# Two-layer encoder trunk on one core: start of the first block, order of the weight casts, pace of the linear heads, last residual

## The chip, the core and the metric

The kernel runs on one core of a Trainium2 chip. A time is the device time of one execution in microseconds (us). The numbers shown for the kernel before are the median of three runs and one execution that was profiled. TensorE is called PE, VectorE DVE, ScalarE ACT, GpSimd POOL and SyncE SP, as the profile calls them. SP, POOL and ACT issue the DMA transfers.

## The reference

Two layers of the same form act on x (512 tokens by 2048, float32):

```python
def hybrid_layer(x, w_in, w_out, g_pre, g_post, w_alpha, b_alpha, g_gla, g_att, rel_bias):
    h = rmsnorm(x, g_pre)
    z = h @ w_in
    gq, gk, gv, gg, ga, aq, ak, av, ag = split_columns(z)
    log_a = log_sigmoid(ga @ w_alpha + b_alpha) / GLA_TAU
    o_gla = gla_chunk_causal(gq, gk, gv, log_a)       # 4 linear heads, state per chunk of 64 tokens
    o_gla = rmsnorm(o_gla, g_gla) * silu(gg)          # norm per head
    o_att = chunk_band_attention(aq, ak, av, rel_bias)
    o_att = rmsnorm(o_att, g_att) * silu(ag)
    y = concatenate([o_gla, o_att]) @ w_out
    return x + rmsnorm(y, g_post)
```

w_in is 2048 by 7184 and w_out 2048 by 2048 for each layer, all float32. The matmuls with w_in and w_out are nearly all of the work.

## The kernel before

**Tiles.** The weights are cut into blocks of 512 output columns, and a block into 8 chunks of 256 rows of the inner dimension, 512 KB each. A chunk lands in a tile `raw` or `H` (two halves of 128 rows side by side: 128 x 1024). Each operand is held as two rounded parts, a high and a low one. ACT makes the high part `wh` of a weight chunk (line 203, a cast), DVE the low part `wl = raw - wh` (line 207); for activations `split` does the same at lines 108 (ACT) and 109 (DVE). A product is then three matmuls: high by high, high by low, low by high. A group of matmuls adds up in a PSUM tile `mm` of 128 x 512.

**Blocks.** `std_gemm` (matmuls at line 323) multiplies a block plainly: gate columns of the attention heads (AG0, AG1) at the start of a layer, and three passes over output blocks at the end of it (NB_IN with four output tiles of 128 tokens; NB_IN+1 in two passes of two tiles). The other blocks go in pairs through `fast_gemm` (lines 399, 409): seven products P1 to P7 of sums of sub-blocks in place of eight. The sums of activations for these are made by `make_sums` (DVE, line 604), split (lines 108, 109), and go through memory. W23 is the pair of output blocks that stands between the two passes over NB_IN+1. It needs the sums of the heads' outputs.

**Weights ahead.** `stream` is the list of all chunks in the order of use. `ahead()` is called when a chunk's matmuls have been written down, and prepares chunks that come later: the load, the cast (`high`) and the subtraction (`low`) of the third chunk on, and the load and cast of the fourth. `wl` has three buffers, `wh` and `raw` four.

**Order.** Each engine runs its own list of instructions in order. The lists are made from the program as written, by a scheduler that moves instructions within their dependencies; `tc.issue_after(x)` adds that an instruction comes behind x. Side work (heads, sums, residuals) is written as generators in `tasks`; the matmul loops advance them by `pump`, `rate` steps for each chunk of matmuls.

**Start.** The transposed input (`in_xt`, tiles H and g, 256 KB each) and the first chunk of AG0 come by SP's queue, two small tables (`gcol`, `cst`) by ACT's. Ten matmuls on zeros (line 654) run on PE until the first operands are there.

**Gates.** When an AG block's sum is complete, ACT reads it from PSUM, scales it by the token's norm and applies SiLU (line 694). The next block's sums use the same PSUM tiles.

**Linear heads.** After the value pair (GV0, GV1) `gla_heads` runs, for four heads and two halves of the tokens: state updates (`outer`, PE, line 1060), reads of the state (`read`, PE, line 1094), sums of squares and norm (`norm`: ACT line 1104, then the power on POOL, line 447), scaling by norm and gate on DVE (line 1112, `gate`), transposition on PE (line 1122, `turn`), scaling by column on ACT (line 1133), and the split into the operand of the output block (tiles a12x, g16, g17, g4, g5). NB_IN takes these operands chunk by chunk; the last two chunks of it need the heads that come last.

**Ends of output blocks.** `project` reads a finished sum: squares on ACT (line 1239), product with the gain on DVE (line 1242). `finish_token` adds up the squares, takes the norm and adds the residual (lines 1255 to 1270). For the last 128 tokens the residual is cut into four pieces of 512: three on DVE (line 1268), one on ACT and POOL (lines 1264, 1265); their stores go out by the queues of SP and ACT in turn.

The functions that the change touches, with their line numbers before it:

## Time and profile before

| what | value |
| --- | --- |
| median of 3 runs | 1643.76 us (1642.11 to 1644.25) |
| profiled execution, its own time | 1642.16 us |
| its span | 1640.4 us |
| PE busy | 1623.6 us, 99% of the span |
| DVE busy | 1227.6 us, 75% |
| ACT busy | 905.5 us, 55% |
| POOL busy | 178.2 us, 11% |
| moved by DMA | 469.59 MB, 286 GB/s on average |

The span runs from the first to the last instruction of the profiled execution; 1.76 us of that execution's time lie outside it. Rows of the timeline give start, duration, engine, line, operation, output<-input, shapes, and in brackets how long the engine had been idle and what ended it. Matmuls overlap: one of 128 x 512 shows some 0.39 us in the trace, while the next one starts some 0.23 us after it.

### The profile page before, as it was taken

How to read it: one execution, taken by the hardware profiler on the slowest of the kernel's cores; microseconds unless marked ns; L12 is line 12 of the kernel's file. 1: busy time of each engine (PE TensorE's matmuls, PEld its weight loads, DVE VectorE, ACT ScalarE, POOL GpSimd, SP SyncE). 2: the span in 40 equal slices, each digit the busy share in tenths (PEclk: the TensorE clock that was granted, in tenths of full speed). 3: DMA queues.
4: the chain of work that ended last, by engine and by line, in shares of the span. 5: the costliest groups of instructions: out<-in, count | busy, mean ns of one | idle time of the engine just before them, and what ended most of it. 6: DMA issues, size and time to landing. Idle time of an engine off the chain costs nothing.

```text
span 1640.4 us, 24886 instructions
## 1 busy us (share of the span) xinstructions
PE 1623.6 (99%) x9030; PEld 1392.1 (85%) x9030; DVE 1227.6 (75%) x1579; ACT 905.5 (55%) x1515; POOL 178.2 (11%) x259
## 2 busy tenths in 40 slices
PE   9999999999999999999999999999999999999997
PEld 7888889999988877688888888899999888776886
DVE  7567776877877876678776676768778778857887
ACT  7444544556666644455784445445556765445553
POOL 1210000001101201310132000000001001013111
PEclk9999999999999999999999999999999999999999
DMA  9979796958858696899779797968588676967996
GB/s 380 350 273 320 281 313 228 309 173 309 293 179 297 206 383 211 283 370 357 285 257 383 267 338 258 322 220 302 192 310 271 207 271 232 357 230 287 394 327 226
DMA packets 150490, 469.59 MB, mean 286 GB/s; under 512 B 16396, under 2 KB 35604, under 8 KB 150368
## 3 DMA queue, kind: packets, MB, share of 16 engines
q1 hardware_dynamic: 127632, 389.36, 68.3%
q0 software_dynamic: 22016, 77.37, 12.1%
q8 instruction: 71, 1.16, 0.3%
q10 hardware_dynamic: 720, 1.28, 0.2%
q14 instruction: 51, 0.42, 0.1%
HBM read 395.83 MB, written 71.06 MB: 285 GB/s over the span
## 4 chain that ended last, share of the span: by engine, by line
PE 97%; DVE 1%; DMA 1%; ACT 1%; issue 0%; DVEq 0%; POOL 0%; SPq 0%; ACTq 0%; POOLq 0%
PE mm L409 45%; PE mm L323 21%; PE mm L399 20%; PE ax L890 2%; PE ax L409 1%; PE ax L873 1%; PE ax L1060 1%; PE ax L721 1%; PE ax L1094 1%; PE ax L853 1%; PE ax L852 1%; PE ax L851 1%; DMA t<-fg 0%; PE ax L921 0%; PE ax L551 0%
## 5 line engine op out<-in xcount | busy, mean ns | idle before, releaser
L409 PE MATMUL mm<-wh,sa 128*128 128x512 f32 x1536 | 484.6, 391 | 0.1
L203 ACT CAST wh<-raw 128x1024 fp32r<-128x1024 f32 x256 | 270.1, 1056 | 262.9 <-PE mm L409 113.3
L207 DVE TENSOR_TENSOR wl<-raw,wh 128x1024 fp32r<-128x1024 f32 x256 | 312.6, 1222 | 122.6 <-PE mm L323 39.0
L203 ACT CAST wh<-H 128x1024 fp32r<-128x1024 f32 x224 | 235.5, 1053 | 221.4 <-PE mm L409 115.1
L207 DVE TENSOR_TENSOR wl<-H,wh 128x1024 fp32r<-128x1024 f32 x224 | 273.8, 1223 | 109.0 <-PE mm L409 50.4
L409 PEld LDWEIGHTS mm<-wh,sa 128*128 128x128 f32 x1536 | 288.0, 188 | 62.3 <-issue 2.4
L409 PE MATMUL mm<-wl,sa 128*128 128x512 f32 x768 | 300.3, 391 | 0.1
L399 PE MATMUL mm<-sa,wh 128*128 128x256 f32 x1280 | 237.1, 285 | 0.0
L399 PEld LDWEIGHTS mm<-sa,wh 128*128 128x128 f32 x1280 | 199.9, 191 | 0.3
L409 PE MATMUL mm<-wh,a 128*128 128x512 f32 x576 | 186.3, 393 | 0.0
L399 PE MATMUL mm<-sa,wl 128*128 128x256 f32 x640 | 180.6, 283 | 0.0
L323 PE MATMUL mm<-wh,a 128*128 128x512 f32 x512 | 167.9, 394 | 4.0 <-ACT a L108 1.2
L409 PEld LDWEIGHTS mm<-wl,sa 128*128 128x128 f32 x768 | 144.2, 188 | 29.6 <-DVE wl L207 0.5
L447 POOL TENSOR_TENSOR sm<-sm,mhalf 128x4 f32<-128x4 f32 (+2 forms) x40 | 67.1, 1678 | 767.1 <-DVE sm L906 542.0
L197 DVE TENSOR_TENSOR H<-H,raw 128x1024 f32<-128x1024 f32 x120 | 146.5, 1221 | 1.7
L409 PEld LDWEIGHTS mm<-wh,a 128*128 128x128 f32 x576 | 108.0, 188 | 22.5
L399 PEld LDWEIGHTS mm<-sa,wl 128*128 128x128 f32 x640 | 122.3, 191 | 0.1
L323 PEld LDWEIGHTS mm<-wh,a 128*128 128x128 f32 x512 | 96.0, 188 | 27.5 <-DVE g L1242 2.0
L409 PE MATMUL mm<-wl,a 128*128 128x512 f32 x288 | 112.9, 392 | 0.0
L323 PE MATMUL mm<-wl,a 128*128 128x512 f32 x256 | 100.4, 392 | 0.5 <-DVE wl L207 0.5
L399 PE MATMUL mm<-a,wh 128*128 128x256 f32 x512 | 94.7, 285 | 0.0
L323 PE MATMUL mm<-wh,sa 128*128 128x512 f32 x256 | 87.0, 396 | 0.0
(203 smaller groups left out, 2324.8 us busy)
## 6 DMA issues: line engine op xcount, KB each, us to landing
raw<-in_w_dram SPq DMA_DIRECT2D x320, 512.0 KB, 5.6
sa<-S SPq DMA_DIRECT2D x192, 512.0 KB, 4.7
H<-in_w_dram SPq DMA_DIRECT2D x56, 512.0 KB, 4.7
sa<-A SPq DMA_DIRECT2D x48, 512.0 KB, 6.5
S<-g POOLq DMA_DIRECT2D x32, 512.0 KB, 7.7
oS<-g POOLq DMA_DIRECT2D x32, 512.0 KB, 6.3
sa<-oS SPq DMA_DIRECT2D x32, 512.0 KB, 5.5
sg<-t POOLq DMA_DIRECT2D x32, 256.0 KB, 5.7
```

Source lines behind the costliest of these rows:

```text
L197: nc.vector.tensor_tensor(out=h, in0=h, in1=r, op=ALU.add)
L203: last_cast[0] = nc.scalar.copy(self.wh, src).ins
L207: last_low[0] = nc.vector.tensor_tensor(out=self.wl, in0=self.src, in1=self.wh.bitcast(F32), op=ALU.subtract).ins
L323: mm = nc.tensor.matmul(pss[o], a[:, part, t], rhs[:, kk, :], start=(i == 0 and kk == 0 and m == 0), stop=(i == n - 1 and kk == 1 and m == 2),
L399: nc.tensor.matmul(dst, lhs[:, kk, f], a[:, part, tok], start=(fresh and kk == 0 and m == 0 and ft % 2 == 0), stop=(c == c_last and kk == ...
L409: nc.tensor.matmul(out_ps[t], a[:, part, tok], rhs[:, kk, :], start=(fresh and kk == 0 and m == 0), stop=(c == c_last and kk == 1 and m == ...
L447: return nc.gpsimd.tensor_tensor(out=out_r, in0=v, in1=mhalf[:, : v.shape[-1]], op=ALU.pow).ins
L721: nc.tensor.matmul(ps[0:96, half * 256 : (half + 1) * 256], wga[kt // 10][:, kt % 10, :], op[:, i, (kt % 2) * 256 : (kt % 2 + 1) * 256], s ...
L851: nc.tensor.matmul(ps[:, :n], self.qh[:, t], self.kh[:, :n], start=True, stop=False)
L852: nc.tensor.matmul(ps[:, :n], self.qh[:, t], self.kl[:, :n], start=False, stop=False)
L853: nc.tensor.matmul(ps[:, :n], self.ql[:, t], self.kh[:, :n], start=False, stop=True)
L890: nc.tensor.matmul(o, self.pt[i][:, j * P : (j + 1) * P], av[hd // 4, j // 2][:, j % 2, (hd % 4) * P : (hd % 4 + 1) * P], start=(j == 0), ...
```

## The change

The changed kernel differs in five places.

1. **First chunk.** The first weight chunk of AG0 is loaded as two halves of 128 x 512. DVE casts the first half, ACT the second, and the subtraction is in two halves too. The table `cst` is loaded by SP's queue behind the first chunk's loads, not by ACT's.
2. **Casts behind gates.** Gate functions return their last instruction, and `high` writes every later cast behind it (`issue_after(last_evac[0])`). Output blocks return nothing, so nothing is added there.
3. **Two chunks ahead.** In `ahead()` the cast and subtraction of plain blocks (`std`) are prepared one chunk later than before: two chunks ahead (casts three, in the second round).
4. **Linear heads.** The pair (GV0, GV1) advances the side work by 4 steps per chunk of matmuls, before 2.
5. **Last residual.** The last 128 tokens' residual is cut into pieces of 512, 512, 512, 256 and 256, all on DVE.

No arithmetic changes; PE has the same matmuls.

```diff
     LEFT = {"P5": "S1", "P6": "S2", "P3": "S4", "P7": "S3", "P4": "A22"}
+    last_evac = [None]
...
             if k == "std":
                 i = done["load"]
-                if i < NCH:
+                if i == 0:
+                    self.raw = rtile("raw")
+                    load_columns(i, 0)
+                    parts = w[self.l, b0, c].rearrange("p (k n) -> p k n", k=2)
+                    for kk in range(2):
+                        with tc.issue_after(last_load[0]):
+                            last_load[0] = nc.sync.dma_start(self.raw[:, kk, :], parts[:, kk, :]).ins
+                    load_columns(i, 1)
+                elif i < NCH:
...
             self.wh = rtile("wh", dtype=F32R)
-            last_cast[0] = nc.scalar.copy(self.wh, src).ins
+            if done["high"] == 0:
+                nc.vector.tensor_copy(self.wh[:, 0, :], src[:, 0, :])
+                last_cast[0] = nc.scalar.copy(self.wh[:, 1, :], src[:, 1, :]).ins
+                return
+            with tc.issue_after(last_evac[0]) if last_evac[0] else nullcontext():
+                last_cast[0] = nc.scalar.copy(self.wh, src).ins
 
         def low(self):
             self.wl = rtile("wl", dtype=F32R, bufs=3)
-            last_low[0] = nc.vector.tensor_tensor(
-                out=self.wl, in0=self.src, in1=self.wh.bitcast(F32), op=ALU.subtract
-            ).ins
+            for kk in range(2) if done["low"] == 0 else (slice(0, 2),):
+                last_low[0] = nc.vector.tensor_tensor(
+                    out=self.wl[:, kk, :], in0=self.src[:, kk, :], in1=self.wh[:, kk, :].bitcast(F32), op=ALU.subtract
+                ).ins
...
         for what, n in (("load", 3), ("high", 3), ("low", 3), ("load", 4), ("high", 4), ("load", 5)):
+            if what != "load" and all(z.kind == "std" for z in stream[i + n - 2 : i + n]):
+                n -= 1
             prepare(what, i + n)
...
             if i == n - 1:
                 last_mm = mm.ins
-                evac(o, pss[o])
+                last_evac[0] = evac(o, pss[o])
                 closing[0] = last_mm
...
     nc.scalar.dma_start(gcol, g_cols)
-    nc.scalar.dma_start(cst, consts)
+    prepare("load", 1)
+    with tc.issue_after(last_load[0]):
+        last_load[0] = nc.sync.dma_start(cst, consts).ins
     prepare("load", 4)
...
         def gate(half, q, t, src, scale=1.0):
             dst = t2()
-            nc.scalar.activation(dst, src, AF.Silu, scale=scale)
+            made_gate = nc.scalar.activation(dst, src, AF.Silu, scale=scale).ins
             nc.gpsimd.dma_start(sg_d[l][half][t * P : (t + 1) * P, q * W : (q + 1) * W], dst)
+            return made_gate
...
-                gate(half, q, o, ps, inv_rms(l, o))
+                return gate(half, q, o, ps, inv_rms(l, o))
...
-        fast_gemm(l, PAIRS[5], gv_consume, rate=2, after=fetch_operands)
+        fast_gemm(l, PAIRS[5], gv_consume, rate=4, after=fetch_operands)
...
-            step = 512 if end else xs[0].shape[-1]
-            for i in range(D // step):
-                h, o = i * step // 1024, i * step % 1024
-                xt, yt = piece(xs, i * step, step), ys[t, h][:, o : o + step]
-                if end and i == 3:
-                    nc.scalar.activation(yt, yt, AF.Copy, scale=r)
-                    nc.gpsimd.tensor_tensor(out=xt, in0=yt, in1=xt, op=ALU.add)
-                else:
-                    with tc.issue_after(last_low[0]):
-                        nc.vector.scalar_tensor_tensor(out=xt, in0=yt, scalar=r, in1=xt, op0=ALU.mult, op1=ALU.add)
+            o = 0
+            for i, n in enumerate((512, 512, 512, 256, 256) if end else (xs[0].shape[-1],) * (D // xs[0].shape[-1])):
+                xt, yt = piece(xs, o, n), ys[t, o // 1024][:, o % 1024 : o % 1024 + n]
+                with tc.issue_after(last_low[0]):
+                    nc.vector.scalar_tensor_tensor(out=xt, in0=yt, scalar=r, in1=xt, op0=ALU.mult, op1=ALU.add)
                 q = (nc.sync, nc.scalar)[i % 2] if last and t > 1 else nc.gpsimd
-                q.dma_start((out if last else x_mid)[t * P : (t + 1) * P, i * step : (i + 1) * step], xt)
+                q.dma_start((out if last else x_mid)[t * P : (t + 1) * P, o : o + n], xt)
+                o += n
                 yield
```

In the built programs the changed kernel's lines have other numbers: 323 becomes 340, 203 becomes 217 (213 and 214 for the halves), 207 becomes 222, 694 becomes 713, 604 becomes 621, 1122 becomes 1142, 1242 becomes 1262. Three places of the instruction lists show what moves.

The first is the start of DVE's list, up to the second `split`: `raw` and `wh`, `wl` are the first weight chunk, `H` the first columns of the input, `a110` their operand. Before:

```order
L566 TENSOR_SCALAR H_3_211<-H_3_211,gcol_202 128x256
L109 TENSOR_TENSOR a110_20_258<-H_3_211,a110_20_258 128x512
L657 CAST later_206<-cst_203 128x128
L207 TENSOR_TENSOR wl_19_254<-raw_4_213,wh_18_252 128x1024
L566 TENSOR_SCALAR g14_5_215<-g14_5_215,gcol_202 128x256
```

And with the change:

```order
L583 TENSOR_SCALAR H_4_211<-H_4_211,gcol_202 128x256
L213 CAST wh_18_253<-raw_3_210 128x512
L222 TENSOR_TENSOR wl_19_256<-raw_3_210,wh_18_253 128x512
L109 TENSOR_TENSOR a110_20_261<-H_4_211,a110_20_261 128x512
L222 TENSOR_TENSOR wl_19_256<-raw_3_210,wh_18_253 128x512
L583 TENSOR_SCALAR g14_5_215<-g14_5_215,gcol_202 128x256
```

DVE now casts and subtracts the first half-chunk by itself, before the low part of the input's operand, and the cast of `cst` has moved behind both subtractions.

The second is ACT's list where AG0 ends and AG1 begins in layer 0: squares of the token norms (lines 460 and 477), the casts of AG1's second to fourth chunk (`wh`), and the four gates. Before:

```order
L460 ACTIVATE t2_88_579,sm_84_571<-sg_79_552 128x512
L108 CAST g4_104_692<-g14_5_215 128x512
L108 CAST g5_105_703<-H_3_211 128x512
L203 CAST wh_106_713<-raw_98_620 128x1024
L677 CAST g13_95_607<-g12_94_606 98x512
L694 ACTIVATE t2_99_646<-mm_14_248,norm_1_207 128x512
L694 ACTIVATE t2_100_663<-mm_15_249,norm_1_207 128x512
L694 ACTIVATE t2_103_688<-mm_16_250,norm_1_207 128x512
L694 ACTIVATE t2_112_725<-mm_17_251,norm_1_207 128x512
L203 CAST wh_110_721<-raw_109_719 128x1024
```

And with the change:

```order
L477 ACTIVATE t2_86_578,sm_82_570<-sg_77_551 128x512
L713 ACTIVATE t2_97_645<-mm_14_249,norm_1_207 128x512
L713 ACTIVATE t2_98_662<-mm_15_250,norm_1_207 128x512
L713 ACTIVATE t2_101_687<-mm_16_251,norm_1_207 128x512
L217 CAST wh_104_712<-raw_73_546 128x1024
L217 CAST wh_108_720<-raw_96_619 128x1024
L713 ACTIVATE t2_110_724<-mm_17_252,norm_1_207 128x512
L217 CAST wh_119_772<-raw_107_718 128x1024
```

Three gates now follow the last squares directly; the casts of AG1's second and third chunk stand behind them. Before, the second chunk's cast (`wh_97`) stood ahead of the last four squares, and the third chunk's ahead of all gates.

The third is PE's list at the end of NB_IN in layer 0: the turns of the last two heads, and the chunks of NB_IN around them. `a120`, `g4`, `a121`, `g5` are operands made from heads, `mm_1225` to `mm_1228` the four sums (`mm_1245` to `mm_1248` with the change). Before:

```order
L323 MATMUL mm_1228_6464<-wl_1282_6739,g4_1315_6903 128x512
L323 MATMUL mm_1228_6464<-wh_1258_6630,g4_1315_6903 128x512
L1122 MATMUL ax_1336_6987<-cst_203,bias_1291_6795 128x128 x4
L1122 MATMUL ax_1346_7030<-cst_203,sg_1312_6887 128x128 x4
L323 MATMUL mm_1225_6461<-wh_1283_6741,a121_1337_6992 128x512
L323 MATMUL mm_1225_6461<-wl_1301_6833,a121_1337_6992 128x512
...
L323 MATMUL mm_1226_6462<-wh_1283_6741,a121_1337_6992 128x512
L323 MATMUL mm_1369_7094<-wh_1302_6835,a111_1150_6131 128x512
```

And with the change:

```order
L1142 MATMUL ax_1325_6902<-cst_203,bias_1283_6716 128x128 x3
L340 MATMUL mm_1246_6540<-wh_1317_6878,a120_1285_6733 128x512
L1142 MATMUL ax_1332_6945<-cst_203,sg_1304_6808 128x128
L340 MATMUL mm_1247_6541<-wh_1317_6878,g4_1307_6830 128x512
L1142 MATMUL ax_1332_6945<-cst_203,sg_1304_6808 128x128 x3
...
L340 MATMUL mm_1245_6539<-wh_1330_6941,a121_1326_6907 128x512
...
L340 MATMUL mm_1246_6540<-wh_1330_6941,a121_1326_6907 128x512
L340 MATMUL mm_1247_6541<-wh_1330_6941,g5_1333_6950 128x512
...
L340 MATMUL mm_1248_6542<-wh_1330_6941,g5_1333_6950 128x512
L340 MATMUL mm_1367_7093<-wh_1336_6983,a111_1150_6134 128x512
```

Before, the last turns stood directly ahead of the matmuls on their result (`a121`), and the next block's first matmul (`mm_1369`) directly behind the first two sums of the last chunk. Now some dozen matmuls on `g4` stand between the last turns and `a121`, and all four sums of the last chunk are done before the next block's first matmul (`mm_1367`).

## The prediction

> **What bounds the kernel now.** I read the page first, then the waits of PE, and then the timeline around each wait.
>
> ```profile
> PE 1623.6 (99%) x9030; PEld 1392.1 (85%) x9030; DVE 1227.6 (75%) x1579; ACT 905.5 (55%) x1515; POOL 178.2 (11%) x259
> 103.53 152.32 PE mm L409 x672
> ```
>
> PE is busy for 1623.6 of the 1640.4 us, and the chain's longest piece, 672 matmuls in 152.32 us, gives 0.2267 us as the pitch of one. The change leaves PE's matmuls as they are, so it can only gain from the 16.8 us in which PE stands idle, and it loses whatever new waits it makes. The waits of PE name most of them (engine and line, what it waited for, total us, times, longest):
>
> ```profile
> PE ax L1122 <- issue: 2.2, 2, 1.1
> PE mm L323 <- ACT a L108: 1.2, 2, 0.6
> PE mm L323 <- DVE g L1242: 1.2, 2, 0.6
> PE mm L323 <- ACT wh L203: 0.8, 1, 0.8
> PE mm L323 <- ACT t L694: 0.8, 1, 0.8
> PE mm L323 <- DVE wl L207: 0.5, 1, 0.5
> PE mm L323 <- ACT g L108: 0.3, 1, 0.3
> ```
>
> The first three lines come twice, once a layer, at the end of the linear heads; the casts `wh` and `wl` are the start, the gate `t L694` is AG0's end. The rest of the idle time is the tail, below. So each wait has its own place, and I price each from its own rows.
>
> **The start.** Rows give start, us, engine, line, operation, tiles and shapes.
>
> ```profile
> 1.58 4.05 PE L654 MATMUL ax<-t 128*128 128x512 bf16 x9
> 3.77 0.35 DVE L566 TENSOR_SCALAR H<-H,gcol 128x256 f32<-128x256 f32 x1 [2.65 <-DMA gcol<-in_g_cols_dram]
> 4.30 0.62 ACT L108 CAST a<-H 128x512 fp32r<-128x512 f32 x1
> 4.95 0.69 DVE L109 TENSOR_TENSOR a<-H,a 128x512 fp32r<-128x512 f32 x1 [0.82 <-ACT a L108]
> 5.31 1.05 ACT L203 CAST wh<-raw 128x1024 fp32r<-128x1024 f32 x1 [0.39 <-DMA raw<-in_w_dram]
> 6.39 1.23 DVE L207 TENSOR_TENSOR wl<-raw,wh 128x1024 fp32r<-128x1024 f32 x1 [0.61 <-ACT wh L203]
> 7.67 0.50 PE L323 MATMUL mm<-wl,a 128*128 128x512 f32 x1 [0.53 <-DVE wl L207]
> 8.01 0.62 PE L323 MATMUL mm<-wh,a 128*128 128x512 f32 x2
> 10.10 1.23 DVE L207 TENSOR_TENSOR wl<-raw,wh 128x1024 fp32r<-128x1024 f32 x1
> ```
>
> The chain is: weights there by 5.31, cast, subtraction, and the third matmul at 7.67, from where PE runs on. The first half is 256 KB at the head of the same queue; at the 419 GB/s of a window below that is 0.6 us sooner than the whole, and `cst` (193 KB, 0.5 us) no longer shares the channel: an estimate of 4.2. DVE then casts it (0.62, as ACT's 128 x 512 does, since no DVE cast of that size is in the trace; bounds 0.35 and 0.69 from the two DVE rows) and subtracts (0.69): `wl` of the half at 5.5. The input's high part is there at 4.92, its low part at 6.2 (DVE, behind the first subtraction), the second half's `wl` at 6.9. PE's zeros end at 5.63; from then the first low half is ready for the third matmul, the input's for the fifth (6.5), the second half's for the eighth (7.2). At the pitch of the zeros (4.05 / 9 = 0.45) the third stands at 6.5, at 0.2267 at 6.1: a gain of 1.2 to 1.6. I take 1.4. The low end is 0.4 (the cold start, below), the high end 1.9, the slack of the second chunk: its subtraction ended at 11.33, and its third matmul came at 13.25.
>
> Slow zeros may mean that the first real matmuls run slowly too. In the trace full pitch is seen from 8.01 on (0.62 for two), and little ran from 5.6 to 6.4, so it doesn't show when the pitch changed. If it is at 8.0, matmuls that now start at 5.63 run at 0.45 for 2.4 us: 1.2 lost of the 1.6.
>
> [...]
>
> **Gates.**
>
> ```profile
> 49.87 1.06 ACT L203 CAST wh<-raw 128x1024 fp32r<-128x1024 f32 x1 [3.29 <-PE mm L323]
> 51.34 1.84 ACT L694 ACTIVATE t<-mm,norm 128x512 f32<-128x512 f32 x3
> 52.08 0.50 PE L323 MATMUL mm<-wh,a 128*128 128x512 f32 x1 [0.78 <-ACT t L694]
> ```
>
> ACT sat behind a cast that waited 3.29 us for PE to free a `wh` buffer; the gates, three of them ready, stood behind it, and AG1's first matmul waited for the first. PE idled 0.78 for it, and after a wait the next matmul follows later (7.67 to 8.01 above is 0.34, not 0.23): 0.9 lost. With three gates ahead of the casts the first is done by about 47 (ACT had idled from 46.6, with its squares done), so the wait goes whole: gain 0.9. What is late next? AG1's second chunk is now cast behind three gates. The third sum ends 12 matmuls before the block does (2.7 us), so this cast ends about 0.6 + 1.06 later, still ahead of the block's end. Its subtraction stands behind a small DVE copy that waits for the block's end, and is done 1.6 us after it; PE's first matmul on it is the 19th of AG1, 4.1 us behind. That covers it by 2.5 us.
>
> **Two chunks ahead.** A `wl` buffer is free only when PE has left the chunk three before, so `wl` can't be made sooner in either kernel; what moves is the place in ACT's and DVE's lists. In the output block NB_IN+1 the list lets the fourth chunk's cast wait for the four squares at the end of NB_IN: 0.6 + 0.2 + 1.05 + 1.22 = 3.1 us behind that end, needed three chunks of 12 matmuls (8.2 us) behind it. So the cover is 5 us, and the price nothing. Bounds: nothing, and the two smallest waits of the table (0.3 and 0.5) in each of the six runs of plain blocks, 4.8. I charge 0.6, two of 0.3.
>
> **Linear heads.** The end of layer 0's heads (the first row is one of the chain, the others are of the timeline):
>
> ```profile
> 679.93 0.44 PE ax L1122 x4
> ...
> 683.99 0.38 ACT L1104 ACTIVATE t<-ax 128x256 bf16<-128x256 f32 x1
> 686.71 1.23 DVE L207 TENSOR_TENSOR wl<-raw,wh 128x1024 fp32r<-128x1024 f32 x1 [1.14 <-PE mm L323]
> 686.74 0.60 PE L1122 MATMUL ax<-cst,bias 128*128 128x128 f32 x4
> 688.43 0.90 PE L1122 MATMUL ax<-cst,sg 128*128 128x128 f32 x4 [1.09 <-issue]
> 689.28 0.62 ACT L108 CAST a<-t 128x512 fp32r<-128x512 f32 x1
> 689.95 0.50 PE L323 MATMUL mm<-wh,a 128*128 128x512 f32 x1 [0.62 <-ACT a L108]
> 692.09 0.60 ACT L1239 ACTIVATE t<-mm 128x512 bf16<-128x512 f32 x1 [2.20 <-PE mm L323]
> 692.57 0.39 PE L323 MATMUL mm<-wh,a 128*128 128x512 f32 x1
> 693.56 0.50 PE L323 MATMUL mm<-wh,a 128*128 128x512 f32 x1 [0.60 <-DVE g L1242]
> ```
>
> The last norm's scaling on DVE stood behind the subtraction of 686.71 (1.14 us of waiting for PE ahead of it), so the second turn came at 688.43, its scaling and cast followed, and the matmuls went on at 689.95. From 686.74 to there PE did two turns of 0.44 (first row): 3.21 - 0.88 = 2.33 us lost. The next block's first matmul then waited for the squares and the product that free its PSUM tile: 693.56 - 692.57 - 0.23 = 0.76. Two slow restarts of 0.11 make 3.3. Layer 1 shows the same waits and 0.3 more for `ACT g L108`: 3.7 with its restart.
>
> In the changed list the last turns stand 12 to 15 matmuls of 128 x 512 (2.7 to 3.4 us) ahead of the matmuls on their result; from a turn to the operand it took 689.95 - 688.43 = 1.52. The next block's first matmul stands 12 matmuls behind the first two sums of the last chunk, 2.7 us, where squares and product took the 1.5 us from 692.09 to 693.56. Both are covered by over 1 us. So I expect 3.3 + 3.7 = 7.0 to go. What remains open is where it reappears:
>
> ```profile
> 700.00:720.00 20.00, 20.00 (x90) 16.53 (x90) 12.43 (x14) 10.41 (x14) 2.16 (x4) 1.00 1.02 392
> 740.00:750.00 10.00, 10.00 (x46) 8.26 (x45) 9.94 (x12) 5.46 (x8) 0.00 (x0) 1.00 1.03 419
> 1555.00:1565.00 10.00, 9.89 (x44) 7.85 (x44) 10.00 (x11) 5.81 (x9) 0.00 (x0) 1.00 0.98 369
> 1562.89 1.22 DVE L207 TENSOR_TENSOR wl<-H,wh 128x1024 fp32r<-128x1024 f32 x1
> 1564.16 0.50 PE L409 MATMUL mm<-wl,sa 128*128 128x512 f32 x1
> ```
>
> These rows are windows (from:to, length, then busy us of PE, PEld, DVE, ACT and POOL, clock, DMA share, GB/s) and two of the timeline. In W23 DVE is busy for 9.94 and 10.00 of 10 us, since the outputs' sums and the sums of weights fall there, and PE takes `wl` 0.05 us after it is made. If PE arrives 3.3 us sooner and DVE doesn't, the gain is given back here. But DVE is busy for 12.43 of 20 us just before, and the changed list has the first sums ahead of the sixth subtraction of NB_IN+1, where they stood behind the second of W23: some 4 subtractions earlier, a pitch of 2.7 us each. They need the heads' outputs, which are sooner too. So I expect DVE to spread this work, and the 7.0 to stay.
>
> **Last residual.**
>
> ```profile
> 1633.68 1.41 DVE L1268 SCALAR_TENSOR_TENSOR bias<-g,sm,bias 128x512 f32<-128x512 f32 x2
> 1634.48 1.74 POOL L1265 TENSOR_TENSOR sg<-g,sg 128x512 f32<-128x512 f32 x1 [0.83 <-ACT g L1264]
> 1635.02 1.75 DVE L1268 SCALAR_TENSOR_TENSOR sg<-g,sm,sg 128x512 f32<-128x512 f32 x1
> 1636.79 0.33 SPq L1270 DMA_DIRECT2D out_dram<-sg  x1
> ```
>
> The third piece on DVE took 1.75 beside POOL's addition, the first two 1.41 together. Without POOL: 1633.68 + 3 x 0.7 + 2 x 0.39 (0.35 for 256 columns in the start's row, and 0.39 by halving) = 1636.5, so the last store starts 0.3 sooner and holds 128 KB, not 256 KB. At 419 GB/s, the best rate of the windows above, 128 KB are 0.3 us. Gain 0.6; low end 0.3 (a short store lands no sooner), high end 0.8.
>
> **Sum.** 1.4 + 0.9 + 7.0 + 0.6 - 0.6 = 9.3. From the profiled execution's own 1642.16 (1.76 more than its span) that is 1632.9. The median before is 1.60 above that execution, so against it I forecast 1643.76 - 9.3 = 1634.5.
>
> **Rivals.**
>
> *Given back in W23.* PE arrives sooner, DVE can't, and each layer's 3.3 and 3.7 come back as waits for `wl`. For it: the 9.94 and 10.00, and the 0.05. Against it: the 12.43 before. It leaves 9.3 - 7.0 = 2.3, 1641.5; given back by half, 1638.0.
>
> *Casts too late: slower.* At the ends of AG blocks the next chunks' casts queue behind the gates, and PE waits for a gate, a cast and a subtraction, 0.6 + 1.06 + 1.23 = 2.9 each. There are five such ends (two in layer 0, three in layer 1), and with one chunk less ahead nothing is in store: 14.5 us against 9.3 + 0.6, slower by 4.6, 1648.4. It decides from the fourth such wait on (9.9 / 2.9 = 3.4). For it: the wait that goes was itself one of ACT's list, and three gates now stand ahead of a cast that stood free. Against it: the 4.1 us of cover counted above.
>
> *Cold start.* The slow pitch lasts until 8.0: the start brings 0.4, and the time is 1635.5. For it: the zeros' 0.45. Against it: nothing in the trace.
>
> *The heads stay late.* The change of pace moves the list, but the operands (gates' loads from memory, states on DVE) come no sooner, and PE waits in the new places: the 7.0 stay lost, the time is as in the first rival, 1641.5. Against it: the changed list has at least 17 matmuls with a read or update between a read and its turn, 3.9 us and more, for squares, norm, scaling and the wait for the turn, which took from 683.99 to 688.43 with 1.14 us in them that DVE spent waiting for PE.
>
> **How the numbers follow.** The forecast has 0.60, with the cold start's 0.10 beside it in the same range of its own, 1631 to 1637. The two ways to lose the heads' gain have 0.22 together: 0.14 by half (1638.0), 0.08 in full. Casts too late has 0.08, of it 0.02 with only three such waits, which cancel the gain. A measurement of this kernel can't tell less than 0.2% (3.3 us) from no change, so what is below 1640.5 counts as faster: 0.70 + 0.14 = 0.84. The full loss and the three waits are within it: 0.10. Slower is 0.06. The range begins at 1630.5: all high ends (1.9 + 0.9 + 7.4 with the waits near 1564 + 0.8 = 11.0, no new wait) give 1632.8, and 2 us are for the spread of the runs before (1642.11 to 1644.25). It ends at 1641.5, where the heads' gain is lost.
>
> **What would show it.** Right: the third matmul near 6.3 in place of 7.67; no `ACT t L694` in PE's waits; none of the first three lines of that list; PE's idle time near 9 of the 16.8, nearly all of it the tail; DVE busier in the 20 us before W23 and no longer full in it; the last store issued near 1627. Wrong: new lines of PE waiting for `wl` or `wh` of plain blocks (casts), PE waiting at W23 for line 222 (given back), or waits for the turns at other places.

## The result and the profile after

In 22 executions of each, side by side, the changed kernel took 1641.72 us (median), the kernel before 1643.93. The ratio is 0.9985, with a 95% interval of 0.9979 to 0.9992: 2.2 us gained where 9.3 were forecast. The interval leaves out 1, but the gain is below the 0.2% (3.3 us) from which the prediction speaks of faster. One of the 22 executions of the changed kernel ran at a granted clock of 0.58, took 2585.85 us and isn't in the ratio; without it the median is 1641.52. The forecast of 1634.5 is wrong, and 1641.72 lies just outside its range, which ended at 1641.5. The profiled execution took 1640.27 us, 1.89 less than that of before, and its span is 1638.3 us, 2.1 less.

From the page of the changed kernel, the line of PE:

```profile
PE 1628.6 (99%) x9030; PEld 1397.8 (85%) x9030; DVE 1227.9 (75%) x1583; ACT 903.3 (55%) x1514; POOL 161.9 (10%) x258
```

And all that is left of its waits of PE (engine and line, what it waited for, us in total, times, longest):

```profile
PE ax L673 <- DVE t L670: 1.2, 1, 1.2
PE mm L340 <- DVE wl L222: 0.3, 1, 0.3
```

The waits that the forecast meant to remove are gone, as it said; the first line here is the wait for the zeros' tile at 1.18, which was there before. But PE's busy time has risen by 5.0 us (from 1623.6), with the same 9030 matmuls. The idle time went down from 16.8 to 9.7 us, nearly all of it the start and the tail, but most of that gain was eaten by matmuls that took longer as a group.

To see where, I number the matmuls of the big products (lines 323, 399 and 409 before; 340, 416 and 426 after), which are 7,584 in both kernels, and compare the starts of those of the same number in the traces. Negative means sooner than in the kernel before, in us. The last three columns belong to experiments below: the changed kernel with the turns of the state update restored ("turns"), with half of the residual's input loaded later ("load"), and with both.

| start of big matmul number | before at | after | turns | load | both |
| --- | --- | --- | --- | --- | --- |
| 25, start of AG0 | 12.79 | -1.34 | -1.38 | -1.06 | -1.34 |
| 193, start of AG1 | 52.08 | -2.25 | -2.27 | -1.99 | -2.36 |
| 2901, ahead of the heads, layer 0 | 585.04 | -2.30 | -2.21 | -1.89 | -2.67 |
| 3265, end of NB_IN, layer 0 | 696.42 | -1.97 | -3.90 | -1.55 | -4.22 |
| 3401, start of W23, layer 0 | 727.25 | -1.31 | +0.56 | -1.55 | -4.22 |
| 4151, layer 1 under way | 912.53 | -1.26 | +1.72 | -1.04 | -2.09 |
| 6693, ahead of the heads, layer 1 | 1400.02 | -1.35 | +1.44 | -0.92 | -1.95 |
| 7057, end of NB_IN, layer 1 | 1511.77 | -1.38 | -0.61 | -0.95 | -4.00 |
| 7193, start of W23, layer 1 | 1542.59 | -1.38 | +1.10 | -0.95 | -4.00 |
| 7584, the last | 1631.66 | -1.80 | +0.68 | -0.27 | -3.59 |

In "after", the start and the gates bring their 2.25. Then comes the section of the heads, 585 to 696, from which 3.3 us were to go in layer 0: it is 0.33 longer than before. Behind it, in NB_IN+1, another 0.66 is lost. In layer 1 the heads bring 0.03 of the forecast 3.7.

What filled the heads' section is seen in the groups of PE's instructions in that section (line, engine, operation, tiles, shapes and count; busy us and mean ns of one). Of the kernel before, from 585 to 727:

```profile
L1060 PE MATMUL ax<-g,g 64*128 64x256 f32 x96 | 9.7, 299 | 0.0
L1094 PE MATMUL ax<-g,g 128*64 128x256 f32 x64 | 8.7, 392 | 0.0
```

And of the changed kernel, from 583 to 726:

```profile
L1080 PE MATMUL ax<-g,g 64*128 64x256 f32 x96 | 13.2, 303 | 0.0
L1114 PE MATMUL ax<-g,g 128*64 128x256 f32 x64 | 9.3, 393 | 0.0
```

These are the 96 matmuls of the state update and the 64 reads. The single update lasts as long as before (299 and 303 ns), but 96 of them cover 13.2 us, where they covered 9.7. If each big matmul and each small one is given the time from its start to the start of the next, the section adds up as follows (us, layer 0):

| matmuls | before | after | difference |
| --- | --- | --- | --- |
| big | 89.02 | 87.89 | -1.13 |
| turns of a head's output, line 1122 / 1142 | 5.42 | 3.08 | -2.34 |
| state update, line 1060 / 1080 | 8.82 | 12.05 | +3.23 |
| reads of the state, line 1094 / 1114 | 8.11 | 8.69 | +0.58 |
| sum | 111.37 | 111.71 | +0.34 |

The waits went, 3.47 us of them (forecast: 3.3). The update took the time back. One update is twelve matmuls on operands of 64 rows, six for each half (`cc` 0 and 1) of a tile of 128 tokens. In the timeline of PE before, a whole unit and the big matmul behind it:

```profile
623.67 0.97 PE L1060 MATMUL ax<-g,g 64*128 64x256 f32 x12
624.57 0.50 PE L409 MATMUL mm<-wh,sa 128*128 128x512 f32 x1
```

In PE's list the sums of such a unit's two halves come in turn (here `ax_1202` and `ax_1203`, first four rows of twelve):

```
L1060 MATMUL ax_1202_6367<-g4_1140_6084,g8_1026_5564 128x256
L1060 MATMUL ax_1203_6368<-g4_1140_6084,g8_1026_5564 128x256
L1060 MATMUL ax_1202_6367<-g6_1141_6085,g8_1026_5564 128x256
L1060 MATMUL ax_1203_6368<-g6_1141_6085,g8_1026_5564 128x256
```

In the changed list six of one half stand together, and the six of the other come later, behind other matmuls:

```
L1080 MATMUL ax_1187_6302<-g4_1140_6087,g8_1026_5567 128x256
L1080 MATMUL ax_1187_6302<-g6_1141_6088,g8_1026_5567 128x256
...
L1080 MATMUL ax_1188_6303<-g4_1140_6087,g8_1026_5567 128x256
L1080 MATMUL ax_1188_6303<-g6_1141_6088,g8_1026_5567 128x256
```

This unit stands in the timeline of the changed kernel so:

```profile
615.25 0.97 PE L1080 MATMUL ax<-g,g 64*128 64x256 f32 x6
616.15 0.72 PE L426 MATMUL mm<-wh,a 128*128 128x512 f32 x2
...
617.74 0.97 PE L1080 MATMUL ax<-g,g 64*128 64x256 f32 x6
618.64 1.08 PE L1114 MATMUL ax<-g,g 128*64 128x256 f32 x8
```

Twelve matmuls whose halves come in turn take 0.90 us (623.67 to 624.57): in the trace they start two at a time, 0.004 us apart, with 0.11 to 0.22 from pair to pair, so the two halves run side by side. Six of one half alone take 0.90 too (615.25 to 616.15), starting one by one with 0.12 to 0.22 between starts, and the other six 0.90 again. In the kernel before one of eight units of a layer is split like this, in the changed one four of eight: the scheduler that makes the lists was free to part the halves, and at the pace of 4 steps it did. Three more split units at 0.90 are 2.7 of the 3.23; the other 0.5 is in two units that still alternate, but of which one or two matmuls now stand apart from the rest (0.2 and 0.3 more). The reads lose their 0.58 in the same way: before, all eight groups of eight stand together and take 1.01 each; now one of them stands as six and two with other matmuls between, 1.01 and 0.58.

The other places, from the timeline of the changed kernel: the start, the first gates, the casts of NB_IN+1 and the end.

```profile
4.80 0.43 DVE L213 CAST wh<-raw 128x512 fp32r<-128x512 f32 x1 [0.55 <-DMA raw<-in_w_dram]
5.38 0.80 PE L340 MATMUL mm<-wh,a 128*128 128x512 f32 x2
6.01 0.73 PE L340 MATMUL mm<-wl,a 128*128 128x512 f32 x2
6.24 0.62 ACT L214 CAST wh<-raw 128x512 fp32r<-128x512 f32 x1 [1.20 <-DMA raw<-in_w_dram]
6.61 1.26 PE L340 MATMUL mm<-wh,a 128*128 128x512 f32 x4
7.71 0.42 PE L340 MATMUL mm<-wl,a 128*128 128x512 f32 x1
...
46.15 1.90 ACT L713 ACTIVATE t<-mm,norm 128x512 f32<-128x512 f32 x3
47.95 1.98 ACT L217 CAST wh<-raw 128x1024 fp32r<-128x1024 f32 x2
...
707.75 1.42 DVE L621 TENSOR_TENSOR t<-t,t 128x512 f32<-128x512 f32 x2 [3.88 <-DMA t<-fg]
708.47 0.62 ACT L108 CAST g<-t 128x512 fp32r<-128x512 f32 x1 [7.10 <-DVE t L621]
709.06 1.05 ACT L217 CAST wh<-raw 128x1024 fp32r<-128x1024 f32 x1
710.46 1.22 DVE L222 TENSOR_TENSOR wl<-raw,wh 128x1024 fp32r<-128x1024 f32 x1
711.74 0.50 PE L340 MATMUL mm<-wl,a 128*128 128x512 f32 x1 [0.35 <-DVE wl L222]
...
1633.21 1.54 DVE L1283 SCALAR_TENSOR_TENSOR sg<-g,sm,sg 128x512 f32<-128x512 f32 x3
1633.99 1.12 SPq L1285 DMA_DIRECT2D out_dram<-sg  x2
```

Near 708 a new chain of waits is seen. DVE's list has the first sums of outputs (L621) ahead of a chunk's subtraction, and waited 3.88 us for their input `t<-fg`, which comes from memory. ACT's cast of such a sum waited 7.10 us, and a weight cast stood behind it (709.06); its subtraction ended at 711.7, and PE waited 0.35 for it. This is the 0.66: the idle time counts from the end of the matmul ahead, which lasts 0.16 beyond the pitch (0.39 and 0.23), and the restart is slow by 0.11 (0.34 to the next start, not 0.23).

### The profile page after: what moved, and what is told of

It reads as the page before. It is cut to its first block, busy times and chain, and to the rows that moved or that the text cites. A ratio compares the mean times of both kernels' runs of the same rounds, so it can differ in the third digit from the quotient of the medians.

```text
span 1638.3 us, 24908 instructions
## 1 busy us (share of the span) xinstructions
PE 1628.6 (99%) x9030; PEld 1397.8 (85%) x9030; DVE 1227.9 (75%) x1583; ACT 903.3 (55%) x1514; POOL 161.9 (10%) x258
## 4 chain that ended last, share of the span: by engine, by line
PE 98%; DMA 1%; DVE 0%; issue 0%; ACT 0%; DVEq 0%; POOLq 0%
PE mm L426 46%; PE mm L340 21%; PE mm L416 20%; PE ax L910 2%; PE ax L1080 1%; PE ax L426 1%; PE ax L893 1%; PE ax L1114 1%; PE ax L741 1%; DMA t<-fg 1%; PE ax L873 1%; PE ax L872 1%; PE ax L871 1%; PE ax L1142 0%; PE ax L941 0%; PE ax L568 0%
## 5 line engine op out<-in xcount | busy, mean ns | idle before, releaser
L222 DVE TENSOR_TENSOR wl<-raw,wh 128x1024 fp32r<-128x1024 f32 (+1 forms) x257 | 312.4, 1217 | 118.8 <-PE mm L426 37.2
L464 POOL TENSOR_TENSOR sm<-sm,mhalf 128x4 f32<-128x4 f32 (+2 forms) x40 | 53.0, 1325 | 770.5 <-DVE sm L926 542.5
```

The lines of the kernel that those rows point to most:

```text
L222: last_low[0] = nc.vector.tensor_tensor(out=self.wl[:, kk, :], in0=self.src[:, kk, :], in1=self.wh[:, kk, :].bitcast(F32), op=ALU.subtract ...
L464: return nc.gpsimd.tensor_tensor(out=out_r, in0=v, in1=mhalf[:, : v.shape[-1]], op=ALU.pow).ins
```

## The experiments

Ratios are against executions of the kernel before on the same chip, with 95% intervals.

**1. The turns restored.** In the changed kernel, the twelve matmuls of an update are tied into one order, so that the halves come in turn. `prev` starts as None.

```diff
                     for i in range(3):
                         for cc in range(2):
-                            nc.tensor.matmul(
+                            with tc.issue_after(prev) if prev else nullcontext():
+                                prev = nc.tensor.matmul(
...
+                                ).ins
```

> The changed kernel, with the 12 matmuls of each state update (outer) written as one chain in which the two 64-row halves alternate. Theory P (pairs): in the changed kernel's trace seven updates per layer-half that stand as six matmuls of one half and then six of the other take 0.90 us per six, and an alternating twelve takes 0.90 us together; all updates of a layer then took 12.06 us, before the change 8.82. Alternating again, they take about 8.2 to 9 us per layer, PE gains 3.0 to 3.8 us per layer, and the time is about 6 us below the changed kernel's: 1641.7 - 6 = 1635.7 against 1643.9 before, ratio about 0.995. Rival W (given back in W23): the heads' gain is lost because PE meets late weights behind the heads; then PE shows new waits for wl where the gain arrives, and the time stays within 2 us of the changed kernel's.

Measured: 1641.5 us, 0.9991 (0.9982 to 1.0000). The heads' section is shorter by 2.0 us in each layer than with the change (table, from number 2901 to 3265 and from 6693 to 7057), so the split is a cause and worth 2 us a layer, less than the 3.0 to 3.8 expected: the tie leaves the first of the twelve by itself in six of the eight units, and one alone takes 0.31. But all of it is lost behind the section, so for the time rival W was right. The two largest waits of PE of this kernel:

```profile
PE mm L340 <- DVE wl L222: 2.6, 3, 0.9
PE mm L340 <- ACT wh L217: 1.7, 2, 1.4
```

and its timeline near 708, in the same places as above:

```profile
693.98 0.54 POOL L1159 DMA_DIRECT2D fg<-t  x1 [1.65 <-ACT t L1261]
698.13 0.54 POOL L1159 DMA_DIRECT2D fg<-t  x1 [1.53 <-ACT wh L217]
708.03 1.42 DVE L621 TENSOR_TENSOR t<-t,t 128x512 f32<-128x512 f32 x2 [6.10 <-DMA t<-fg]
708.76 0.62 ACT L108 CAST g<-t 128x512 fp32r<-128x512 f32 x1 [9.32 <-DVE t L621]
709.30 1.04 ACT L217 CAST wh<-raw 128x1024 fp32r<-128x1024 f32 x1
710.40 0.73 PE L340 MATMUL mm<-wh,a 128*128 128x512 f32 x2 [1.40 <-ACT wh L217]
712.02 0.60 PE L340 MATMUL mm<-wl,a 128*128 128x512 f32 x1 [0.89 <-DVE wl L222]
```

PE comes 2 us sooner, the sum's input lands at the same time (708.03 and 707.75), and PE waits 2.3 us. A window then shows what more it costs (from:to, length; busy us of PE, PEld, DVE, ACT, POOL; clock; DMA share; GB/s):

```profile
700.00:710.00 10.00, 9.00 (x40) 7.13 (x38) 3.16 (x4) 1.24 (x2) 0.00 (x0) 1.00 1.04 404
710.00:720.00 10.00, 8.71 (x30) 6.76 (x31) 8.84 (x12) 7.19 (x11) 2.14 (x4) 0.83 1.03 397
```

The granted clock is 0.83 in the window behind the waits, 1.7 us of the 10: it is 0.50 from 712.3 to 715.6 and 1.00 on both sides. So 4.5 us are lost between the heads and W23 in layer 0.

**2. The turns broken in the kernel before.** The update is written half by half and tied.

```diff
-                for tt in range(2):
-                    for cc in range(2):
+                for cc in range(2):
+                    for tt in range(2):
...
```

> The kernel before, with the state updates written half by half (six matmuls of one 64-row half, then six of the other); nothing else is changed. Theory P: of eight updates per layer, six that stood alternating in one group, or nearly so, cost 0.9 us more each; 5 to 6.5 us per layer, 10 to 13 us in all: about 1655, slower by 0.6 to 0.8%. Theory W and the theory that only the number of switches between small and large matmuls counts: the same number of matmuls in groups as large as before, no change beyond 2 us.

Measured: 1651.74 us, 1.0049 (1.0035 to 1.0063). PE falls behind by 3.9 us (layer 0) and 3.6 (layer 1), all of it inside the two heads' sections, with the same waits of PE as before but one of 0.3. The turns are worth time by themselves. Here the loss stays, while in experiment 1 the gain did not. A unit costs less than the 0.9 expected, though. Its twelve matmuls, six of one half and directly behind them six of the other, take 1.25 us from the first to the next big matmul:

```profile
613.39 1.32 PE L1060 MATMUL ax<-g,g 64*128 64x256 f32 x12
614.64 0.50 PE L409 MATMUL mm<-wh,a 128*128 128x512 f32 x1
```

Three of the second half start before the last of the first: the signal that the trace has on the last of six is here on the ninth start. So in this list some partners overlapped without being direct neighbours (1.25 for the twelve, where two sixes at 0.90 would be 1.80); in the changed kernel, with other matmuls between the two sixes, each six took its whole 0.90. In layer 0 the updates take 2.66 us more than before, and the reads 1.14, since two of their groups are now parted.

**3. Which edit breaks the turns: the pace.** One line, in the kernel before (rate 2 to 4) and in the changed kernel (4 to 2).

```diff
-        fast_gemm(l, PAIRS[5], gv_consume, rate=2, after=fetch_operands)
+        fast_gemm(l, PAIRS[5], gv_consume, rate=4, after=fetch_operands)
```

> The kernel before, with the heads' pace of 4 alone. Prediction on record: 7.0 us faster, 1636.9. Theory P: the waits at the heads' end go (3.3 and 3.7 us), the updates lose their pairs (3.2 per layer): between 0 and 1.5 us faster, ratio 0.999 to 1.000, and the updates take 12 us per layer in the trace. Theory W: the updates stay as in the trace before (8.8 us per layer), and the loss stands as waits for wl in W23.

> The changed kernel with the heads' pace of 2 as before: start, casts and last residual alone. Theory P: the start's 1.2, the gates' 1.05 and the tail's 0.3 remain, the heads' waits (3.3 and 3.7) are back and the updates take 8.8 us per layer: 2.5 us faster than before, ratio 0.9985, the same as the whole change. If the pace of 4 brought a net gain of 3 us or more, this kernel would be within 1 us of the time before.

The pace of 4 alone makes the kernel before slower: 1653.74 us, 1.0066 (1.0052 to 1.0080), where theory P had 0 to 1.5 us gained. Its list has four of eight units split. Taken out of the change, it leaves a faster kernel than the change by the medians: 1639.09 us, 0.9974 (0.9963 to 0.9984; the intervals touch), where theory P had 0.9985. There one of eight units is split, PE's busy time is 1623.6 us again, and the old waits at the heads' end are back. The largest waits of PE with the pace alone:

```profile
PE mm L323 <- ACT wh L203: 4.8, 3, 2.1
PE mm L323 <- DVE wl L207: 1.8, 2, 0.9
```

and in the changed kernel without it:

```profile
PE ax L1142 <- issue: 2.6, 2, 1.5
PE mm L340 <- DVE g L1262: 1.2, 2, 0.6
```

With the pace alone 5.2 and 4.5 us are lost between number 3265 and 3401 and in layer 1, where the change itself lost 0.66 and nothing. The other edit that bears on that place is the third, two chunks ahead.

**4. Casts three chunks ahead again.** In the changed kernel:

```diff
             if what != "load" and all(z.kind == "std" for z in stream[i + n - 2 : i + n]):
-                n -= 1
+                n -= 0
```

> The changed kernel with the casts and subtractions of plain blocks again three (four) chunks ahead; the gates' order, the start, the pace of 4 and the residual stay. In the kernel before with the pace of 4 alone, 5.2 and 4.5 us were lost between the heads and W23. If preparing one chunk later is what took this away in the changed kernel (0.7 and 0), the loss comes back: about 1641.7 + 8 = 1650. If the pace alone decides (or the gates' order), the time stays within 2 us of the changed kernel's.

Measured: 1650.66 us, 1.0041 (1.0026 to 1.0055). Between the heads and W23 5.0 us are lost in layer 0 and 4.2 in layer 1. So the edit that I charged 0.6 for its small waits is worth some 4 us a layer once the pace is 4. How it does that is open. From the first sums on, DVE's and ACT's lists have the same order there in both kernels. But SP issues the load of the sums' input at 697.94 where the change has 695.36, and it lands at 712.2, there at 707.7: 4.5 us later, while PE is only 1.6 us later. DVE waits 6.82 us for it, where it waited 3.88.

**5. The sums held back.** On top of experiment 1, the side work in NB_IN+1 starts 12 (first) or 8 (second) steps later.

```diff
-        std_gemm(l, NB_IN + 1, (0, 1), OO, operand_out, out_evac(1), rate=0.6, lag=2)
+        std_gemm(l, NB_IN + 1, (0, 1), OO, operand_out, out_evac(1), rate=0.6, skip=12, lag=2)
```

> The changed kernel with the state updates alternating, and the side work held back for 12 of the 16 steps of NB_IN+1's first pass, so that the first sums of the heads' outputs stand on DVE behind the second subtraction of W23, not ahead of the sixth of NB_IN+1. Theory L (a sum that waits for a load stands ahead of a weight): with alternating updates alone the heads' section gained 1.7 and 2.0 us over the changed kernel's loss, and 4.5 and 1.7 us were lost behind it where DVE waited 6.1 us for a load of the sums and PE for the subtraction behind it. Then these 6 us come back, but for up to 1 us where DVE is full in W23 as before: about 1636.5, ratio 0.996, no wait of PE for wl between 700 and 716. Rival D (the weights' own loads are late, since DMA is full there): PE waits for wh or wl at the same place, with ACT or DVE waiting for raw, and the time stays at 1640 to 1641.5.

> The same with the side work held back for 8 of 16 steps: the first two sums stand around the seventh subtraction. Theory L: the first wait of DVE falls one chunk (2.7 us) later, so most of the waits go and some 0 to 1.5 us are left: 1636 to 1638. Rival D: as with 12 steps, no gain.

Measured: 1645.68 us, 1.0006 (0.9997 to 1.0015), and 1645.02, 1.0003 (0.9994 to 1.0013). Theory L missed both times, but its mechanism is seen. With 12 steps PE is 4.37 us ahead at W23's start: the late sums were what held it in NB_IN+1. This lead is lost in W23, where the operands made from these sums are late, once a layer:

```profile
PE mm L426 <- DMA sa<-oS: 5.7, 2, 2.9
```

With 8 steps part is lost in each place. Moving the work about in the list only moved the wait; the sums have to be ready sooner.

**6. The turns at the old pace.** Experiment 1 with rate 2.

> The changed kernel with the heads' pace of 2 as before and alternating updates. Theory P: of the eight updates of a layer only one stood split at that pace, so 0.9 us per layer go, against the changed kernel at pace 2 (0.9974 of before): 1637.3, ratio 0.9963. If splitting costs nothing, the ratio stays 0.9974.

Measured: 1645.65 us, 1.0005 (0.9996 to 1.0015), slower than the same pace without the tie (0.9974, above). Theory P missed: the updates of layer 0 take 8.86 us, and 8.83 without the tie, since it leaves the first of the twelve by itself in three units. The lists come out differently, with new waits inside the heads:

```profile
PE mm L340 <- ACT g L108: 3.5, 2, 1.8
PE ax L1144 <- DVE sg L1134: 2.0, 2, 1.0
```

So the tie isn't a gain by itself; at this pace it puts PE in front of operands that aren't made.

**7. The sums' input sooner: the residual's input loaded later.** At the heads' end POOL asks for 4 MB of the residual's input (`x`), while the channel is full (in experiment 1 its share is 1.01 from 680 to 700 and 1.04 from 700 to 720), and the stores of the heads' outputs (`fg<-t`) stand behind these loads in POOL's list. The loaded input is first used at 790.07, in the kernel before. First all of it is asked for behind the store of W23's last sum, on top of experiment 1, and on the changed kernel at the old pace:

```diff
-        with tc.issue_after(last_norm[0]):
-            xs0 = load_tokens(0, x_src, nc.gpsimd)
-            xs1 = load_tokens(1, x_src, nc.gpsimd)
...
         def fetch_last(k, c):
+            if (k, c) == ("P5", C_END[-1]):
+                with tc.issue_after(last_put[0]):
+                    xs[0] = load_tokens(0, x_src, nc.gpsimd)
+                    xs[1] = load_tokens(1, x_src, nc.gpsimd)
```

> The changed kernel with the update's halves in turn, and the 4 MB of the residual's input, which POOL asks for at the heads' end (685 to 700), asked for behind the store of the last sum of weights in W23. Theory (DMA crowding makes the block NB_IN+1 late: its input's load took 12 us with the channel full from 680 to 720): the load of the input lands about 5 us sooner, the waits for the weights' low half at line 222 near 710 and 1528 go (4.5 in layer 0, 1.7 in layer 1, of which 1.8 to 2 of slow clock), and the kernel runs 6 us ahead of the pairs alone: 1635.5 against 1641.5. Rival (DVE's list is the bound; the first sums stand ahead of the subtraction and last as long): the waits stay within 0.5 of what they were, 1641.5. Second rival (the load moves to where the channel is just as full, 740 to 770, and the sums' operands or the residual wait): the gain at 710 is seen and 3 us or more are lost per layer between 740 and 790, 1641 to 1644.

> The changed kernel at the old pace of the last fast block (rate 2) with the residual's input asked for behind the store of the last sum in W23. At the old pace only 0.7 us were lost in the section behind the heads (the waits for a turn, a cast and a norm are still there, 3 to 4 in all). Theory of crowding: 0.7 in layer 0 goes, nothing in layer 1, the time is 1638.4 against 1639.1 without it. Rival (the channel is as full at 740 to 770): 1 to 3 per layer lost there, 1641 to 1645.

With the turns: 1641.23 us, 0.9986 (0.9977 to 0.9995). Nothing is lost between the heads and W23 any more (PE is 3.71 ahead at number 3401 and 3.40 at 7193), and then 1.5 near 742 to 747 in layer 0 and 4.1 from 1557 on in layer 1, in W23. That is the second rival. At the old pace 1651.63 us, 1.0055 (1.0042 to 1.0068), a miss: in W23 alone 6.1 and 6.3 us are lost, with this line among the waits of PE:

```profile
PE mm L427 <- DMA sa<-oS: 7.1, 5, 2.3
```

Then only the second half (2 MB), at the same place or at the first chunk of W23's last product:

```diff
             if (k, c) == ("P4", C_END[0]):
                 with tc.issue_after(last_put[0]):
                     xs[1] = load_tokens(1, x_src, nc.gpsimd)
```

> As the run before with the halves in turn and the residual's input asked for later, but only the second half of that input (2 MB, for the last two token tiles) is moved behind the last sum's store; the first half stays at the heads' end. Theory of crowding: the channel has 2 MB less at 680 to 720 and 2 MB less at 740 to 770 than in the two cases; the loss at 710 falls from 4.5 to 1 or less in layer 0 and from 1.7 to nothing in layer 1, and that behind it from 1.9 and 4.1 to 1 or less. PE is then 3 to 4 us ahead of the kernel before at the end of layer 0 and 3 to 5 at its end: 1639 to 1640 against 1643.5. Rival (each of the two places is full by itself, and half is as bad as the whole): 4 or more lost per layer, no better than 1641.2.

> The same with the second half asked for still later, at the first chunk of W23's last product (P4), where no sum's operand is loaded any more. Theory of crowding: nothing is lost at 740 to 770, and the time is 0 to 1.5 us below that of the other place, 1638 to 1640. Rival (the next layer's norm, which reads this half, comes late behind 800): 1 to 3 us lost between 800 and 860 in layer 0, 1641 or more.

Measured: 1637.41 us, 0.9966 (0.9953 to 0.9979), and 1637.06, 0.9963 (0.9949 to 0.9977), below what the theory of crowding expected. The two edits turn out to be one kernel: the instruction lists of all engines are the same but for buffer numbers. The loads leave POOL from 724.24 and from 722.92 on, 0.1 us ahead of W23's first matmul in each, and the loads of sums' operands still come behind them (from 738.64 to 763.98 in the second). So a still later place was not tried, and the two medians are one measurement taken twice. This version beats both kernels; against the changed kernel at the old pace (0.9974) the intervals overlap. The table's last column is the second of the two. Its timeline:

```profile
685.28 0.56 POOL L1160 DMA_DIRECT2D fg<-t  x1
687.83 0.55 POOL L1160 DMA_DIRECT2D fg<-t  x1 [2.00 <-ACT t L1156]
701.54 1.41 DVE L622 TENSOR_TENSOR t<-t,t 128x512 f32<-128x512 f32 x2
702.79 1.05 ACT L218 CAST wh<-raw 128x1024 fp32r<-128x1024 f32 x1
```

The first sums are made 6.5 us sooner than in experiment 1 (701.54 and 708.03), and the same weight cast 6.5 us sooner (702.79 and 709.30). The stores of the outputs leave POOL 8.7 and 10.3 us sooner. Both the room in the channel and the shorter list of POOL have a part. The load that the first sums wait for is issued at the same time in experiment 1 and here:

```profile
693.43 0.33 SPq L658 DMA_DIRECT2D t<-fg  x1
693.12 0.34 SPq L659 DMA_DIRECT2D t<-fg  x1
```

It landed 14.5 us later there and 8.1 here, so for the first sums it is the transfer that got shorter. The next load of outputs follows directly on the landing of the first of the stores (at 705.98 there, 698.32 here), and this store took no less time than before (12.0 and 13.0 us): for the later sums it is POOL's list. Not all is gained: of the 4.22 us that PE is ahead at W23's start in layer 0, 0.8 are lost near 745 at a wait for `wl`, and 1.2 near 860; the first of the two loses 0.7 and nothing.

**8. The load alone.** The changed kernel with that last edit and the turns as the change left them, and the kernel before with it.

> The changed kernel with only the later load (the second half of the residual's input at the first chunk of W23's last product); the halves of the state update stand as the change left them, six after six in 4 of 8 units. Theory (the broken turns cost PE time of their own, 2 us a layer as in the kernel before against the pairs alone, and the full channel the rest): PE reaches the heads' end 2 us a layer later than with both edits, the time is 4 us above theirs, 1641. Rival (the turns cost nothing once the channel has room, because the loads of the output set the end of the heads): 1637 to 1638, as with both.

> The kernel before with only the later load. Theory (its waits at the heads' end come from the order of its lists, and behind them it loses nothing but 0.4 us near 1564): 0 to 0.6 gained, 1643 to 1643.5. Rival (the waits at the heads' end are the full channel's as well, since the load and the stores of the output share it): 2 us or more gained, 1641 or less.

In the changed kernel: 1641.42 us, 0.9985 (0.9977 to 0.9994), as the theory had it. PE loses nothing between the heads and W23, and in the heads it gains as little as in the changed kernel (0.34 lost, 0.03 gained). So of four versions, the change has 0.9985, with the turns 0.9991, with the load 0.9985, with both 0.9963: neither brings a measurable gain over the change, both together 4.4 us over either at the medians (1641.5 and 1641.42 against 1637.06). In the kernel before the load makes it slower, 1646.15 us, 1.0017 (1.0008 to 1.0026), which neither theory had: the waits at the heads' end stay nearly as they were (so these 2 MB aren't their cause), but 2.9 us are lost near 750 in layer 0, with the wait

```profile
PE mm L410 <- DMA sa<-oS: 3.0, 2, 1.8
```

and 3.2 in layer 1. (This trace is of an execution of 1649.6 us, 3.4 above the median, where the losses must be smaller.) Its first sums are made from 713.44 on, 12 us later than with both edits (701.54):

```profile
713.44 0.69 DVE L605 TENSOR_TENSOR t<-t,t 128x512 f32<-128x512 f32 x1 [3.68 <-DMA t<-fg]
```

That alone isn't the cause: without the edit they are made later still, from 716.63 on, and PE doesn't wait in W23 of layer 0. With it, the 2 MB stand behind the last store of a sum, so they leave POOL from 733.13 on (725.59 in the changed kernel), and the channel's share from 750 to 760 is 1.01 where it was 0.89. That the sums' operands are late for this reason is argued, not shown.

## Why the prediction was wrong

**Start, 1.4: right, by errors that cancel in part.** The trace gives 1.34 at the 25th matmul. The third matmul came at 6.01, sooner than the 6.1 to 6.5 of the forecast, because the first started at 5.38 and not at the zeros' end in the trace (5.63), and because DVE's cast took 0.43, not 0.62, so that the first low half was made by 5.95. But the landing was sized wrong: the first half was there at 4.8 (estimated 4.2), the second at 6.24, when the whole chunk had been there by 5.31. So the second half's cast and the matmuls up to 7.71 were late and took back 0.3. The cold start fell: the matmul of 5.38 lasted until the next at some 0.40, and those from 5.78 on ran at full pitch (0.23 from 5.78 to 6.01) but for waits and the slow restarts behind them (0.33 from 6.01 to 6.35). (The zeros stand 0.43 apart; the 0.45 of the prediction counts the last one's whole duration.) With the slow pitch over by 5.8, the 1.2 us that the forecast's low end set aside for it were not lost.

**Gates, 0.9: right.** 0.91 between the 25th and the 193rd matmul. The first gate started at 46.15, and AG1's casts behind three gates (47.95) held up nothing.

**Two chunks ahead, -0.6: the sum right by luck, the place wrong.** There is one wait, by which 0.66 is lost, in NB_IN+1, at a point where the list now has the first sums ahead of a subtraction. I had seen that row of the list and read it as relief for DVE in W23. I had not priced that these sums wait for their input from memory, and that everything behind them in DVE's and ACT's lists waits too. And I had charged this edit with a price only, where it saved 4 us a layer at the pace of 4 (experiment 4).

**Linear heads, 7.0: wrong, and this is the forecast's error.** The waits went as said: 2.34 of the turns, 1.13 around the big matmuls, 3.47 for the 3.3 of layer 0. The step that failed is "The change leaves PE's matmuls as they are, so it can only gain from the 16.8 us in which PE stands idle". It took the number of matmuls for their time. The change of pace leaves the count and changes their order, and the update's matmuls ran in pairs where the halves came in turn (twelve in 0.90 us) and not where they were parted (six in 0.90): +3.23, and +0.58 for the reads, of which a group was parted too. What came out is +0.33 in layer 0 and -0.03 in layer 1. Neither rival on the heads was this: *the heads stay late* gave nearly the same time, 1641.5, but by waits that were to remain at other places, and none did; the number agrees by chance.

Had the pairs held, the forecast would still have been wrong. Experiment 1 brought 2 us a layer back, and the section behind the heads took 4.5 us in layer 0 and 1.7 in layer 1: the wait for the sums' input, the chunk behind it, and the clock. *Given back in W23* had the right kind of mechanism (PE sooner, the chunk's low part not) in the wrong place: not in W23 for DVE being full, but in NB_IN+1 for DVE standing idle behind a transfer (3.88 us, and 6.10 in experiment 1). This is that stretch in the changed kernel:

```profile
700.00:720.00 20.00, 19.65 (x87) 15.95 (x86) 14.65 (x19) 10.64 (x17) 2.14 (x4) 1.00 1.03 390
```

DVE is busy for 14.65 of 20 us there, where it was 12.43; PE is the one that waits, and the channel is full (a share of 1.03). In the kernel before, the sums stood later in DVE's list (made from 716.63 on) and PE came later, so that nothing waited there; experiment 5 shows that the place in the list is enough to keep the wait out of NB_IN+1. With both causes removed 1637.06 us remain, against the forecast's 1634.5: the heads then bring 1.55 and 2.05 of the 3.3 and 3.7, since the update still takes 9.99 where it took 8.82, and the reads their 8.68. Another 2.1 us of layer 0's gain are lost from W23's start to number 4151 (table).

**Last residual, 0.6: the low end.** From the last matmul's end to the end of the span it was 8.35 us, and is 8.06: 0.3. DVE does the pieces as forecast (1.54 for the last three). The store of 128 KB at the end is what brought next to nothing: the issue of the last store moved by 2.0 us (from 1636.79 to 1634.77, which is 0.34, one issue, ahead of the end of the two at 1633.99), of which 1.8 are PE's, and the end by 2.1.

**The wait near 1564** went, 0.42, as the forecast's high end allowed.

*Casts too late: slower* fell: no chunk behind a gate was late. The lower end of the range is 1630.8 by the prediction's own terms (1632.8 less 2), not 1630.5; nothing hangs on it.

## What to carry to other kernels

When a change of pace or order is priced, don't take the count of an engine's instructions for their time: here the same 9030 matmuls kept PE busy for 1623.6 us before and for 1628.6 after. Where a trace shows small matmuls running side by side, as it did here (twelve in 0.90 us, and six in 0.90), look in the new list whether the partners still stand close together. The slack of the waits removed here went to the next transfer (in experiment 1, 2.0 us gained over the change in layer 0's heads and 4.5 lost behind them): name what that stretch loads, in which list the loads stand and what stands behind them, before the gain is kept in the sum. And two causes in a row hid each other: singly removed they brought no measurable gain here, together 4.4 us.

## What the runs showed of the hardware

The matmuls of the update, on 64 rows, ran two at a time where those of the two halves came in turn: 12 in 0.90 us, in six pairs that start 0.004 us apart (623.67, in the kernel before). Six of one half with other matmuls around them took 0.90 too, starting one by one (615.25, in the changed kernel). Six of one half and directly behind them six of the other took 1.25 (experiment 2), the first three of the second six starting before the last of the first.

Two waits of 1.40 and 0.89 us, 1.6 us apart, were followed by a window of 10 us at a clock of 0.83 (experiment 1): 3.4 us at half clock, which cost 1.7. PE had been idle for 2.3 us in all. The length of a wait did not decide it in these runs. In experiment 5 with 12 steps PE waits 2.86 us in each layer: behind the wait in layer 1 the clock is 0.50 from 1564.3 to 1567.6, behind the one in layer 0 it stays at 1.00 (746.8 to 753.6). In the kernel at the old pace with all of the load moved, PE waited 2.26 us at a stretch near 754, and that window's clock stayed at 1.00:

```profile
740.00:760.00 20.00, 16.24 (x70) 12.53 (x69) 16.58 (x17) 10.01 (x14) 1.83 (x4) 1.00 1.03 407
```

The first weight chunk, loaded in halves, was there later at its end than the whole had been: 6.24 against 5.31 us, though its first half was there 0.5 sooner (4.80). Its second half was issued at 1.66, the whole at 1.18.
